# A hybrid decoder layer on one core: token sums in later heads, a fourth place for gate weight sums, closing steps beside the next head, scores two steps behind

## The chip, the core and the metric

The kernel runs on one core of a Trainium2 chip. A core has five engines that run beside each other, each with its own instruction order: TensorE (PE, matrix products into PSUM), VectorE (DVE), ScalarE (ACT), GpSimd (POOL) and SyncE (SP), whose queue issues nearly all DMA transfers here. An engine that waits for one instruction holds all that stand behind it. The metric is the device time of one execution in microseconds (us).

## What is computed

One layer of a decoder on 1024 tokens of width 1024, with 16 learned tokens put in front. Everything is float32. Two attention branches of four heads each read the same normalised rows; their outputs are gated, merged and projected, and a gated feed-forward part with a causal convolution follows:

```
h = concat(meta, x)                                   # 1040 rows
p = rms_norm(h) @ w_in + b_in                         # split into 13 parts
log_a = log_sigmoid(g_lr @ gla_w_gate + gla_b_gate) / 16
o_gla = head_rms(gla_chunked(g_q, g_k, g_v, log_a)) * silu(g_r)          # 4 heads
o_ml  = head_rms(mlstm_chunked(silu(conv(m_q, m_k)), m_v, m_i, m_f)) * sigmoid(m_o)   # 4 heads
h = h + (sigmoid(gate_a) * (o_gla @ w_bg) + sigmoid(gate_b) * (o_ml @ w_bm)) @ w_out
h = h + (silu(gate) * up) @ w_down,   gate, up = split(conv(rms_norm(h) @ w_up))
return rms_norm(h)[16:]
```

## The kernel before

**Products.** To keep float32 precision each operand is split into a high and a low part (`wH`, `wL`; `xH`, `xL`), and a product is three matmuls: high by high, high by low, low by high. ACT makes the high part with a copy, DVE the low part with a subtraction. The functions are `prep` (L99) for weights and `proj_cm` (L150) and `proj_v` (L176) for the projections: `proj_cm` goes in three pieces of 24 matmuls of some 346 columns (tile `pj`), `proj_v` in one short and eight long pieces of 24 matmuls of 256 columns (tile `pv`).

**Order.** The kernel is written against a layer that assigns buffers, places waits, and orders the instructions of each engine by priority and its own estimate of time, so an engine's order isn't that of the source. `issue_after` sets a lower bound for the place of an instruction. Buffers are named by tag; a tag with `bufs=2` has two places, and a new tile waits until the tile that had its place has been read by all its readers, DMA stores among them.

**Head stage.** There are eight heads, 0 to 3 of the first kind (`gla`, L570), 4 to 7 of the second (`mlstm`, L774). `head_proj(s)` (L417) makes the keys, queries and values of head s on PE. The rest of a head is a generator that `yield`s between its steps. `main` (L901) runs the projections, and for each projection piece it takes `PACE` = 1.7 steps from the list `side` (L888), so that a head's steps run beside the next head's projections. The loop at the end of the head stage is

```
main(head_proj(0))
for s in range(8):
    side.append((gla if s < 4 else mlstm)(s))
    if s > 3: token_sums(s - 4)
    if s < 7: main(head_proj(s + 1))
```

In `gla`, seven levels (`level`, L637) prepare decayed keys and queries `pk` for block sizes b = 1 to 64. A level has subtractions on DVE (L660, L661), an exponential on ACT (L662), products with the keys on POOL (L664, two for b under 32) and one with the queries on DVE (L665). Four small matmuls then give the scores of that level (`sc`, L601), which DVE copies under a mask (L618). In the source the scores of one level come after the next level. A head ends with `post` (L540): DVE scales the output rows `or` by a reciprocal root that POOL computes (L545), PE transposes them (`ot`, L554), ACT copies them to `of` (L556), and SP stores them to `osc`.

`token_sums(k)` (L456) makes on POOL four sums and differences of the input blocks (two of 1026 columns at L461, four of 514 at L466) and stores them to `tsc` (L468), for the gate stage. Its tiles `xa`, `xb` have the tag `r` (two places), `tx` the tag `gst` (one place).

**Gate stage.** The remaining projections (26 gates of 128 columns) are made in 13 rounds of two, each as a two by two block product with seven instead of eight block products (`piece`, L936; PSUM tiles Vg, Xg, Yg, Zg). `gate_weights(q)` (L984) loads the two weight blocks (`gw`), and makes their sums `gsA`, `gsB` and the high and low parts (`gHA`, `gLA`, `gHSA`, `gLSA`, `gHSB`, `gLSB`, `gA`) in four steps, which the loop takes one at a time. The parts A1, SA and SB take turns in three places in `wp`. The results of a round stand in `gu` (two places for each of the two gates). `gate_finish(q)` (L1039), called in round q + 1, loads the head outputs for gates of the first eight rounds (`go`, from `osc`, tag `o`, one place), applies silu or sigmoid on ACT (L1047), multiplies on DVE (L1048) and stores (`otd`); for the other gates it only stores. After each of the rounds 0 to 10 the loop calls `half_sums` (L1051) twice: it loads a quarter of a block of the down projection's weights (tile `ts`, tag `ts`, one place, two transfers), makes four differences on DVE (L1057) and stores them with two transfers (`tdn`, L1059), for the end of the kernel.

After that come the merge, the output projection, the feed-forward part (`up`, L933 again) and the down projection, which the change doesn't touch.

Of the kernel before, what the change touches and what calls it, by code (L numbers as in the profile page):

```python
# [9 lines left out]
F32 = mybir.dt.float32  # L10
# [7 lines left out]
P = 128  # L18
# [27 lines left out]
def hybrid_kernel(ctx, tc, x, meta, norm_mix, w_in, b_in, gla_w_gate, gla_b_gate, gla_norm,  # L46
# [370 lines left out]
    def head_proj(s):  # L417
        h = s % 4
        hh = heads.setdefault(s, {})
        bB = hd.tile([P, DV], F32, name=f"bB{s}", tag="bB", bufs=2)  # L420
        nc.sync.dma_start(bB, rowb(b_in, (O_GV if s < 4 else O_MV) + DV * h, DV))
        if s < 4:
            pk = key_proj(s) if s != 1 else iter(())
            qT = hh["q"] = hd.tile([P, T + 3], F32, name=f"qT{s}", tag="q", bufs=2)
            pq = proj_cm(uq[s], TH_POST if s else SEG_POST, T0, lambda p, t0, n: nc.scalar.activation(
                qT[:, t0:t0 + n], p, AF.Identity, bias=cc(C_GQ + h), scale=QS))
            if s == 0:
                yield from together(pk, pq, key_proj(1))
                yield from proj_cm(uk["lr"], TH_ALL, 0, lambda p, t0, n: nc.scalar.activation(
                    raw_s[0:96, t0:t0 + n], p[0:96, :], AF.Identity, bias=bsm[0:96]))  # L430
            else:
                yield from pk
                yield from pq
        else:
            kT = hd.tile([P, T + 3], F32, name=f"kT{s}", tag="k", bufs=2)
            qT = hd.tile([P, T + 3], F32, name=f"qT{s}", tag="q", bufs=2)
            hh["k"], hh["q"] = kT, qT
            for z, u, c in ((kT, uk[s], C_MK), (qT, uq[s], C_MQ)):
                nc.gpsimd.memset(z[:, 0:3], 0.0)
                yield from proj_cm(u, TH_ALL, 0, lambda p, t0, n, z=z, c=c: nc.scalar.activation(  # L440
                    z[:, 3 + t0:3 + t0 + n], p, AF.Identity, bias=cc(c + h)))
        vt = hd.tile([P, NC + 1, DV + 1], F32, name=f"v{s}", tag="v", bufs=2)
        if s >= 4:
            nc.gpsimd.memset(vt[:, :, DV:DV + 1], 1.0)
        hh["v"] = vt
        yield from proj_v(uv[s], bB, vt)
# [93 lines left out]
    def post(s, o, om, sc, ncols):  # L540
# [7 lines left out]
        yield  # L548
        for j in range(2):
            of = hd.tile([P, T], F32, name=f"of{s}_{j}", tag="of", bufs=2)  # L550
# [19 lines left out]
    def gla(s):  # L570
# [66 lines left out]
        def level(b):  # L637
# [18 lines left out]
            else:  # L656
# [6 lines left out]
                for e, k, _ in early:  # L663
                    nc.gpsimd.tensor_tensor(e, e, k, OP.mult)  # L664
# [3 lines left out]
        pk = level(1)  # L668
        yield
        yield  # L670
        for b in (2, 4, 8, 16, 32, 64):
            nk = level(b)
            if b == 64:
                yield
                turn()
                yield
                scores_diagonal()
                scores_large(pk, 32)
            else:
                scores_small(pk, b // 2)  # L680
            pk = nk
            yield
# [88 lines left out]
        yield from post(s, o, om[:, :DV], sc, [cc(C_GN + j) for j in range(2)])  # L771


    def mlstm(s):  # L774
# [110 lines left out]
        yield from post(s, o, om[:, :DV], sc, [cc(C_MN + 2 * h + j) for j in range(2)])  # L885


    side = []  # L888

    def advance():  # L890
        while side:
            try:
                next(side[0])
                return
            except StopIteration:
                side.pop(0)

    PACE = 1.7
# [13 lines left out]
    main(head_proj(0))  # L912
    for s in range(8):
        side.append((gla if s < 4 else mlstm)(s))
        if s == 3:
            side.append(small_rows())
        if s > 3:
            token_sums(s - 4)
        if s < 7:
            main(head_proj(s + 1))  # L920
    for j in TAIL:
        main(merge_gate_b(j))
    while side:
        advance()
# [59 lines left out]
    def gate_weights(q):  # L984
# [4 lines left out]
        sa, sb = (gs.tile([P, NK, P], F32, name=f"gs{x}{q}", tag=f"S{x}") for x in "AB")  # L989

# [4 lines left out]
        def two(src, name):  # L995
            h, l = (wp.tile([P, NK, P], F32R, name=f"g{p}{name}_{q}", tag="w" + p) for p in "HL")
            split(src, h, l)
            return [(h[:, 4 * i:4 * i + 4], l[:, 4 * i:4 * i + 4]) for i in range(2)]
        a = WP[q] = {}
        a["A11"], a["A12"] = two(rg, "A1")  # L1000
        yield
        nc.vector.tensor_tensor(sa[:, 0:4], ru[:, 0:4], ru[:, 4:8], OP.add)
        nc.vector.tensor_tensor(sa[:, 4:8], rg[:, 0:4], ru[:, 0:4], OP.subtract)
        a["S1"], a["S3"] = two(sa, "SA")
        yield
        nc.vector.tensor_tensor(sb[:, 0:4], sa[:, 0:4], rg[:, 0:4], OP.subtract)
        nc.vector.tensor_tensor(sb[:, 4:8], rg[:, 4:8], sb[:, 0:4], OP.subtract)
        a["S2"], a["S4"] = two(sb, "SB")
        yield
        t = gs.tile([P, NK, P], F32R, name=f"gA22_{q}", tag="A22")  # L1010
# [3 lines left out]

    wsteps = [gate_weights(q) for q in range(NG)]
# [35 lines left out]
    def half_sums(m, c):  # L1051
        t = gs.tile([P, 4, 256], F32, name=f"ts{m}{c}", tag="ts")
# [17 lines left out]
    weights_step(0)  # L1070
    u2 = wp.tile([P, T], F32, name="gu2", tag="gst", bufs=1)[:, :2 * W0].rearrange("p (a b) -> p a b", b=W0)
    behind_ = None
    for q in range(NG):
        gu[q] = [gs.tile([P, T], F32, name=f"gu{i}{q}", tag=f"u{i}", bufs=2) for i in range(2)]
        for p in range(2):
# [9 lines left out]
            if p == 0 and q:  # L1085
                weights_step(q)
                weights_step(q)
                gate_finish(q - 1)
# [660 lines left out]
```

## Time and profile before

| | us |
|---|---|
| three runs | 2021.89, 2028.81, 2032.42 (median 2028.81) |
| the profiled execution | 2011.35 |
| its span, first to last instruction | 2009.6 |
| mean granted TensorE clock | 0.976 of full speed |

In the rows of the profile "A <- B: t, n, longest" means that A sat idle t us in n places until B ended; a row of the timeline has start, duration, engine, line, operation, tiles, and in brackets the idle time before it and what ended it. SPq rows are the issues of transfers. A row of a stretch ("from:to length, ...") has the busy time and instructions of PE, weight loads, DVE, ACT and POOL, then the granted clock, the busy share of the DMA engines and GB/s.

### The profile page before, as it was taken

The page shows a single profiled execution, that of the slowest core. Times are in us where ns is not written, and L with a number is a line of the kernel's source. Part 1 is how long each engine was busy: PE and PEld are TensorE (multiplying, and loading weights), DVE is VectorE, ACT ScalarE, POOL GpSimd, SP SyncE. Part 2 cuts the span into 40 slices and gives each one's busy share as a digit, 9 for nine tenths or more (in the row PEclk, how much of TensorE's full clock was granted, in tenths as well). Part 3 has the DMA queues.
Part 4 walks back from the last instruction along what each step waited for, and adds up shares of the span by engine and source line. Part 5 has one row for each costly group of instructions (what it writes and reads, how often), then busy time and mean ns, then how long its engine had stood idle before and what let it go on. Part 6 is the DMA issues. An engine that isn't in the chain of part 4 may idle for free. (4 is left out here: it accounts for less than half of the span.)

```text
span 2009.6 us, 32599 instructions
## 1 busy us (share of the span) xinstructions
PE 1895.8 (94%) x13377; PEld 1807.0 (90%) x13377; DVE 1227.3 (61%) x1902; ACT 827.7 (41%) x1280; POOL 242.2 (12%) x213
## 2 busy tenths in 40 slices
PE   8699899889999998989999999999999999999998
PEld 8688888788999997988999999999999999987776
DVE  6163655756444266665543244778878887886767
ACT  5134444555433343332243133544444444455564
POOL 5610211200000000000000000002222322200000
PEclk8899999999999998999999999999999999999999
DMA  5311010212221277776584243333333333378794
GB/s 177 98 35 45 22 56 22 56 43 77 76 74 53 61 222 208 225 210 202 171 272 164 63 135 117 107 116 120 101 111 117 121 101 111 110 255 300 280 379 164
DMA packets 237376, 270.02 MB, mean 134 GB/s; under 512 B 13422, under 2 KB 195200, under 8 KB 237227
## 3 DMA queue, kind: packets, MB, share of 16 engines
q1 hardware_dynamic: 235387, 266.09, 41.2%
q8 instruction: 105, 1.72, 0.3%
q10 hardware_dynamic: 1840, 1.85, 0.3%
q14 instruction: 44, 0.36, 0.1%
HBM read 198.33 MB, written 69.57 MB: 133 GB/s over the span
## 5 line engine op out<-in xcount | busy, mean ns | idle before, releaser
L205 DVE TENSOR_TENSOR v<-pv,bB 128x256 f32<-128x256 f32 x64 | 27.0, 422 | 95.5 <-PE pv L201 95.4
L201 PE MATMUL pv<-wH_mv,xH 128*128 128x256 f32 x256 | 76.4, 298 | 0.0
L201 PE MATMUL pv<-wH_gv,xH 128*128 128x256 f32 x256 | 75.6, 295 | 0.0
L201 PE MATMUL pv<-wH_mv,xL 128*128 128x256 f32 x256 | 74.2, 290 | 0.0
L201 PE MATMUL pv<-wL_mv,xH 128*128 128x256 f32 x256 | 73.7, 288 | 0.0
L201 PE MATMUL pv<-wH_gv,xL 128*128 128x256 f32 x256 | 72.7, 284 | 0.0
L201 PE MATMUL pv<-wL_gv,xH 128*128 128x256 f32 x256 | 72.4, 283 | 0.0
L1396 PE MATMUL po<-wH_wo,yH 128*128 128x256 f32 x256 | 72.2, 282 | 0.1
L1396 PE MATMUL po<-wL_wo,yH 128*128 128x256 f32 x256 | 71.6, 280 | 0.3 <-DVE wL_wo L107 0.3
L1396 PE MATMUL po<-wH_wo,yL 128*128 128x256 f32 x256 | 71.8, 281 | 0.0
L664 POOL TENSOR_TENSOR pk<-pk,kT 128x256 f32<-128x256 f32 (+1 forms) x40 | 47.6, 1210 | 158.3 <-ACT pk L662 96.1
L1344 DVE SCALAR_TENSOR_TENSOR cv<-u,fc,cv 128x1024 f32<-128x1024 f32 x44 | 65.3, 1484 | 0.4
L1136 PE MATMUL bg<-ogH,wH_bg 128*128 128x342 f32 x192 | 61.5, 320 | 1.5 <-ACT gb L450 1.5
L1057 DVE TENSOR_TENSOR ts<-ts 128x256 f32<-128x256 f32 x88 | 37.1, 421 | 40.5 <-DMA ts<-in_ffn_w_down_dram 38.4
L1136 PE MATMUL bm<-omH,wH_bm 128*128 128x342 f32 x192 | 61.4, 320 | 0.0
L1136 PE MATMUL bg<-ogL,wH_bg 128*128 128x342 f32 x192 | 61.4, 320 | 0.0
L1136 PE MATMUL bm<-omH,wL_bm 128*128 128x342 f32 x192 | 61.3, 319 | 0.0
L1136 PE MATMUL bg<-ogH,wL_bg 128*128 128x342 f32 x192 | 61.3, 319 | 0.0
L1136 PE MATMUL bm<-omL,wH_bm 128*128 128x342 f32 x192 | 61.3, 319 | 0.0
L1309 POOL TENSOR_TENSOR SB<-SA,rg 128x512 f32<-128x512 f32 x20 | 32.1, 1607 | 235.9 <-issue 114.1
L933 PE MATMUL Xg<-TH,gLSB 128*128 128x258 f32 (+1 forms) x104 | 32.7, 315 | 25.6 <-DVE gLSB L993 25.4
L601 PE MATMUL sc<-pk 128*128 128x128 f32 x224 | 32.6, 291 | 24.2 <-POOL pk L664 12.3
(737 smaller groups left out, 7403.7 us busy)
## 6 DMA issues: line engine op xcount, KB each, us to landing
gw<-in_w_in_dram SPq DMA_DIRECT2D x26, 512.0 KB, 5.3
ts<-in_ffn_w_down_dram SPq DMA_DIRECT2D x44, 256.0 KB, 3.2
tdn<-ts SPq DMA_DIRECT2D x44, 256.0 KB, 4.3
rg<-in_ffn_w_up_dram SPq DMA_DIRECT2D x22, 512.0 KB, 3.7
ru<-in_ffn_w_up_dram SPq DMA_DIRECT2D x22, 512.0 KB, 3.6
adr<-s SPq DMA_DIRECT2D x40, 256.0 KB, 2.8
rd<-in_ffn_w_down_dram SPq DMA_DIRECT2D x20, 512.0 KB, 8.1
do<-tdn SPq DMA_DIRECT2D x18, 512.0 KB, 8.0
```

Of the source, the lines that this page charges most:

```text
L201: nc.tensor.matmul(pt[:, :DV], a[:, k, t0:t0 + P], b[:, k % 4, :], start=(i == 0), stop=(i == 3 * NK - 1))
L205: nc.vector.tensor_tensor(vt[:n, c, :DV], pt[:n, :DV], bB[:n, :], OP.add)
L601: nc.tensor.matmul(pt[:, i, :], pk[:, P * i:P * (i + 1)], pk[:, 512 + P * i:512 + P * (i + 1)], start=True, stop=True)
L664: nc.gpsimd.tensor_tensor(e, e, k, OP.mult)
L933: nc.tensor.matmul(out[:, :n], x[:, k, :], y[:, k, :], start=start and k == 0 and j == 0, stop=stop and k == 3 and j == 2, skip_group_chec ...
L1057: nc.vector.tensor_tensor(t[:, o], t[:, a], t[:, b], OP.subtract)
L1136: nc.tensor.matmul(pt[:, i, :n], a[:, k, :], b[k][:, t0:t0 + n], start=(k == 0 and j == 0), stop=(k == NK - 1 and j == 2))
L1309: late.tensor_tensor(sb[:, 0:4], sa[:, 0:4], rg[:, 0:4], OP.subtract)
L1344: nc.vector.scalar_tensor_tensor(y, u[:, j:SEQ + j], fc[:, j, jj:jj + 1], y, OP.mult, OP.add)
L1396: nc.tensor.matmul(pt[:, :DV], a, b[:, k % 4, :], start=(k == 0 and i == 0), stop=(k == NK - 1 and i == len(terms) - 1))
```

## The change

1. `head_proj` is cut in two. A head's own steps now begin after its keys and queries, beside its own values (`value_proj`) and the next head's keys and queries. `PACE` goes from 1.7 to 1.2.
2. `post` is no longer the end of a head's generator but goes to a second list, `closing`, from which each `advance` takes one step besides one of `side`. It has one empty step more, and `of` moves from tag `of` to tag `r`, where the token sums have their tiles.
3. `token_sums` is held back by `issue_after` behind the clearing of the query tile of heads 4 to 7.
4. In `gla` a level's scores come two levels later, and the second of the two early products goes to DVE.
5. In the gate stage every fourth of the parts A1, SA, SB gets a place of its own (`w4`), the sums are made in the loaded blocks instead of `gsA` and `gsB`, and the steps of a round's weights begin one half round earlier.
6. The tile of `half_sums` takes the tag `o` of `gate_finish`'s `go`.

```diff
--- before.py
+++ after.py
@@ -414,11 +414,9 @@
         return proj_cm(uk[s], TH_ALL if s > 1 else SEG_ALL, 0, lambda p, t0, n: nc.scalar.activation(
             kT[:, t0:t0 + n], p, AF.Identity, bias=cc(C_GK + s)))
 
-    def head_proj(s):
+    def key_query_proj(s):
         h = s % 4
         hh = heads.setdefault(s, {})
-        bB = hd.tile([P, DV], F32, name=f"bB{s}", tag="bB", bufs=2)
-        nc.sync.dma_start(bB, rowb(b_in, (O_GV if s < 4 else O_MV) + DV * h, DV))
         if s < 4:
             pk = key_proj(s) if s != 1 else iter(())
             qT = hh["q"] = hd.tile([P, T + 3], F32, name=f"qT{s}", tag="q", bufs=2)
@@ -436,13 +434,17 @@
             qT = hd.tile([P, T + 3], F32, name=f"qT{s}", tag="q", bufs=2)
             hh["k"], hh["q"] = kT, qT
             for z, u, c in ((kT, uk[s], C_MK), (qT, uq[s], C_MQ)):
-                nc.gpsimd.memset(z[:, 0:3], 0.0)
+                hh["mark"] = nc.gpsimd.memset(z[:, 0:3], 0.0)
                 yield from proj_cm(u, TH_ALL, 0, lambda p, t0, n, z=z, c=c: nc.scalar.activation(
                     z[:, 3 + t0:3 + t0 + n], p, AF.Identity, bias=cc(c + h)))
+
+    def value_proj(s):
+        bB = hd.tile([P, DV], F32, name=f"bB{s}", tag="bB", bufs=2)
+        nc.sync.dma_start(bB, rowb(b_in, (O_GV if s < 4 else O_MV) + DV * (s % 4), DV))
         vt = hd.tile([P, NC + 1, DV + 1], F32, name=f"v{s}", tag="v", bufs=2)
         if s >= 4:
             nc.gpsimd.memset(vt[:, :, DV:DV + 1], 1.0)
-        hh["v"] = vt
+        heads[s]["v"] = vt
         yield from proj_v(uv[s], bB, vt)
 
     def merge_gate_b(j, bank=None):
@@ -546,8 +548,9 @@
         nc.vector.tensor_scalar(om, om, sc[:2, 0:1], None, OP.mult)
         yield
         yield
+        yield
         for j in range(2):
-            of = hd.tile([P, T], F32, name=f"of{s}_{j}", tag="of", bufs=2)
+            of = hd.tile([P, T], F32, name=f"of{s}_{j}", tag="r", bufs=2)
             for gi in range(2):
                 tp = ps.tile([P, 4, P], F32, name=f"ot{s}_{j}_{gi}", tag="s", bufs=3)
                 for i in range(4):
@@ -660,26 +663,27 @@
                     nc.vector.tensor_tensor(e, t[..., b - 1:b].to_broadcast(t.shape), t, OP.subtract)
                 nc.vector.tensor_tensor(pl, b4[:, :, 1, :], ref, OP.subtract)
                 nc.scalar.activation(pk[:, :SEQ], pk[:, :SEQ], AF.Exp, scale=1.0 / 16)
-                for e, k, _ in early:
-                    nc.gpsimd.tensor_tensor(e, e, k, OP.mult)
+                for eng, (e, k, _) in zip((nc.gpsimd, nc.vector), early):
+                    eng.tensor_tensor(e, e, k, OP.mult)
             nc.vector.tensor_tensor(pl, pl, lv(qv, b)[:, :, 1, :], OP.mult)
             return pk
 
-        pk = level(1)
-        yield
-        yield
-        for b in (2, 4, 8, 16, 32, 64):
-            nk = level(b)
-            if b == 64:
-                yield
-                turn()
-                yield
-                scores_diagonal()
-                scores_large(pk, 32)
-            else:
-                scores_small(pk, b // 2)
-            pk = nk
+        made = []
+        for b in (1, 2, 4, 8, 16, 32, 64):
+            made.append((b, level(b)))
+            if len(made) > 2:
+                c, pk = made.pop(0)
+                scores_small(pk, c)
             yield
+        yield
+        c, pk = made.pop(0)
+        assert c == 32
+        turn()
+        yield
+        scores_diagonal()
+        scores_large(pk, 32)
+        (_, pk), = made
+        yield
 
 
         kh = wtile(f"kh{s}")
@@ -768,7 +772,7 @@
                 nc.scalar.activation(junk[:, :DV], o(c), AF.Square, accum_out=ss[:, c + 1:c + 2])
             yield
         sc = rstd_of(ss, DV, NC + 1, hd, f"rs{s}")
-        yield from post(s, o, om[:, :DV], sc, [cc(C_GN + j) for j in range(2)])
+        closing.append(post(s, o, om[:, :DV], sc, [cc(C_GN + j) for j in range(2)]))
 
 
     def mlstm(s):
@@ -882,20 +886,27 @@
         nc.vector.tensor_tensor(ss, ss, rc, OP.mult)
         sc = rstd_of(ss, DV, NC + 1, hd, f"rs{s}")
         nc.vector.tensor_tensor(sc, sc, rc, OP.mult)
-        yield from post(s, o, om[:, :DV], sc, [cc(C_MN + 2 * h + j) for j in range(2)])
-
-
-    side = []
+        closing.append(post(s, o, om[:, :DV], sc, [cc(C_MN + 2 * h + j) for j in range(2)]))
+
+
+    side, closing = [], []
+
+    def step(gens):
+        if gens:
+            try:
+                next(gens[0])
+            except StopIteration:
+                gens.pop(0)
+                return False
+        return True
 
     def advance():
-        while side:
-            try:
-                next(side[0])
-                return
-            except StopIteration:
-                side.pop(0)
-
-    PACE = 1.7
+        step(closing)
+        while side and not step(side):
+            pass
+
+
+    PACE = 1.2
     due = [0.0]
 
     def main(gen, pace=PACE):
@@ -909,18 +920,20 @@
     NP2 = NJ // 2
     tdn = [dram.tile([NP2, P, 2, 512], F32, name=f"tdn{i}") for i in range(2)]
 
-    main(head_proj(0))
+    main(key_query_proj(0))
     for s in range(8):
         side.append((gla if s < 4 else mlstm)(s))
         if s == 3:
             side.append(small_rows())
         if s > 3:
-            token_sums(s - 4)
+            with tc.issue_after(heads[s]["mark"].ins):
+                token_sums(s - 4)
+        main(value_proj(s))
         if s < 7:
-            main(head_proj(s + 1))
+            main(key_query_proj(s + 1))
     for j in TAIL:
         main(merge_gate_b(j))
-    while side:
+    while side or closing:
         advance()
     heads_ctx.close()
 
@@ -986,32 +999,43 @@
         rg, ru = (wp.tile([P, NK, P], F32, name=f"gw{i}{q}", tag="wr", bufs=2) for i in range(2))
         for r, g in ((rg, GATES[2 * q]), (ru, GATES[2 * q + 1])):
             nc.sync.dma_start(r, wsrc(w_in, 0, NK, g[0], P))
-        sa, sb = (gs.tile([P, NK, P], F32, name=f"gs{x}{q}", tag=f"S{x}") for x in "AB")
-
         def split(src, h, l):
             nc.scalar.activation(h, src, AF.Copy)
             nc.vector.tensor_tensor(l, src, h.bitcast(F32), OP.subtract)
 
-        def two(src, name):
-            h, l = (wp.tile([P, NK, P], F32R, name=f"g{p}{name}_{q}", tag="w" + p) for p in "HL")
-            split(src, h, l)
-            return [(h[:, 4 * i:4 * i + 4], l[:, 4 * i:4 * i + 4]) for i in range(2)]
+        def place(name):
+            nonlocal ngw
+            ngw += 1
+            if ngw % 4 == 0:
+                return [gs.tile([P, NK, P], F32R, name=f"g{p}{name}_{q}", tag="w4" + p) for p in "HL"]
+            return [wp.tile([P, NK, P], F32R, name=f"g{p}{name}_{q}", tag="w" + p) for p in "HL"]
+
+        def halves(t):
+            return [(t[0][:, 4 * i:4 * i + 4], t[1][:, 4 * i:4 * i + 4]) for i in range(2)]
         a = WP[q] = {}
-        a["A11"], a["A12"] = two(rg, "A1")
-        yield
-        nc.vector.tensor_tensor(sa[:, 0:4], ru[:, 0:4], ru[:, 4:8], OP.add)
-        nc.vector.tensor_tensor(sa[:, 4:8], rg[:, 0:4], ru[:, 0:4], OP.subtract)
-        a["S1"], a["S3"] = two(sa, "SA")
-        yield
-        nc.vector.tensor_tensor(sb[:, 0:4], sa[:, 0:4], rg[:, 0:4], OP.subtract)
-        nc.vector.tensor_tensor(sb[:, 4:8], rg[:, 4:8], sb[:, 0:4], OP.subtract)
-        a["S2"], a["S4"] = two(sb, "SB")
-        yield
-        t = gs.tile([P, NK, P], F32R, name=f"gA22_{q}", tag="A22")
+        t = place("A1")
+        split(rg, *t)
+        a["A11"], a["A12"] = halves(t)
+        yield
+        s3 = gs.tile([P, 4, P], F32, name=f"gS3{q}", tag="S3")
+        nc.vector.tensor_tensor(s3, rg[:, 0:4], ru[:, 0:4], OP.subtract)
+        nc.vector.tensor_tensor(ru[:, 0:4], ru[:, 0:4], ru[:, 4:8], OP.add)
+        a["S1"], a["S3"] = halves(place("SA"))
+        split(ru[:, 0:4], *a["S1"])
+        split(s3, *a["S3"])
+        yield
+        nc.vector.tensor_tensor(rg[:, 0:4], ru[:, 0:4], rg[:, 0:4], OP.subtract)
+        nc.vector.tensor_tensor(rg[:, 4:8], rg[:, 4:8], rg[:, 0:4], OP.subtract)
+        t = place("SB")
+        split(rg, *t)
+        a["S2"], a["S4"] = halves(t)
+        yield
+        t = gs.tile([P, NK, P], F32R, name=f"gA22{q}", tag="A22")
         a["A22"] = t[:, 0:4], t[:, 4:8]
         split(ru[:, 4:8], *a["A22"])
         yield
 
+    ngw = 0
     wsteps = [gate_weights(q) for q in range(NG)]
 
     def weights_step(q):
@@ -1049,7 +1073,7 @@
             nc.sync.dma_start(otd[g][j], u[:, :NP])
 
     def half_sums(m, c):
-        t = gs.tile([P, 4, 256], F32, name=f"ts{m}{c}", tag="ts")
+        t = gs.tile([P, 4, 256], F32, name=f"ts{m}{c}", tag="o")
         for k in range(2):
             nc.sync.dma_start(t[:, 2 * k:2 * k + 2], w_dn[P * (2 * m + k):P * (2 * m + k + 1), :].rearrange(
                 "p (i n) -> p i n", i=2)[:, :, 256 * c:256 * c + 256])
@@ -1067,7 +1091,6 @@
             weights_step(0)
     for j in COVER:
         main(merge_gate_b(j, gate_bank(f"pc{j}")))
-    weights_step(0)
     u2 = wp.tile([P, T], F32, name="gu2", tag="gst", bufs=1)[:, :2 * W0].rearrange("p (a b) -> p a b", b=W0)
     behind_ = None
     for q in range(NG):
@@ -1082,10 +1105,11 @@
                 weights_step(q + 1)
             if behind_:
                 next(behind_)
-            if p == 0 and q:
+            if p == 0:
                 weights_step(q)
-                weights_step(q)
-                gate_finish(q - 1)
+                if q:
+                    gate_finish(q - 1)
+                weights_step(q + 1)
             next(g)
             behind_ = g
         if q < NP2:
```

## The prediction

> **What bounds the kernel now.** I read the page first, then PE's own waits, then the two places that these name.
>
> ```profile
> span 2009.6 us, 32599 instructions
> PE 1895.8 (94%) x13377; PEld 1807.0 (90%) x13377; DVE 1227.3 (61%) x1902; ACT 827.7 (41%) x1280; POOL 242.2 (12%) x213
> ...
> PE Xg L933 <- DVE gLSB L993: 25.4, 8, 6.9
> PE pj L158 <- ACT kT L414: 16.4, 1, 16.4
> PE ot L554 <- DVE or L545: 12.6, 5, 6.0
> PE sc L601 <- POOL pk L664: 12.3, 8, 3.1
> PE sc L601 <- DVE pk L665: 9.3, 8, 2.1
> ...
> PE sc L601 <- DVE A L588: 2.0, 2, 1.8
> ...
> PE Yg L933 <- DVE TL L1028: 1.9, 1, 1.9
> ...
> PE Yg L933 <- ACT TH L1027: 1.8, 1, 1.8
> ```
>
> PE sets the pace: 94% busy, 113.8 us idle. The waits are a list of what can be had: 16.4 us once in the head stage, 36.2 us spread over it (12.6 + 12.3 + 9.3 + 2.0), 25.4 us in the gate stage, 3.7 us at its start. The work of PE is the same before and after, so the change can win little more than these 82 us and the slow clock behind them. The first place is the single wait:
>
> ```profile
> 75.24 0.32 SPq L468 DMA_DIRECT2D tsc<-xb  x1
> 75.66 0.39 SPq L102 DMA_DIRECT2D wr_gq<-in_w_in_dram  x1
> ...
> 80.96 1.06 ACT L106 ACTIVATE wH_gq<-wr_gq 128x1024 fp32r<-128x1024 f32 x1 [24.05 <-DMA wr_gq<-in_w_in_dram]
> ...
> 82.43 0.66 PE L158 MATMUL pj<-xH,w_lr 128*128 128x346 f32 x1 [16.37 <-ACT kT L414]
> ```
>
> Although the program asks for token sums at heads 4 to 7, they run at 40 to 91 us. SP's queue is in order: the load of head 1's query weights stands behind stores that wait for POOL, ACT stands at the split of these weights, and behind that split stands the eviction that PE needs.
>
> The second place is the gate stage. These are SP's issues in one round (a pair of gates), DVE's longest wait, and mean rounds:
>
> ```profile
> 801.10 1.26 SPq L1054 DMA_DIRECT2D ts<-in_ffn_w_down_dram  x2
> ...
> 806.87 1.49 SPq L1059 DMA_DIRECT2D tdn<-ts  x2
> 808.41 0.60 SPq L1046 DMA_DIRECT2D go<-oscg  x1
> 811.17 1.25 SPq L1054 DMA_DIRECT2D ts<-in_ffn_w_down_dram  x2
> ...
> 819.68 0.57 SPq L1059 DMA_DIRECT2D tdn<-ts  x1
> 820.30 0.72 SPq L1046 DMA_DIRECT2D go<-oscg  x1
> 825.34 1.73 SPq L1054 DMA_DIRECT2D ts<-in_ffn_w_down_dram  x2
> ...
> 789.99 0.43 DVE L1057 TENSOR_TENSOR ts<-ts 128x256 f32<-128x256 f32 x1 [7.25 <-DMA ts<-in_ffn_w_down_dram]
> ...
> 732.95:903.27 170.32, 149.96 (x1178) 148.16 (x1177) 108.32 (x197) 54.11 (x73) 0.00 (x0) 0.93 0.72 212
> 903.27:974.03 70.76, 63.91 (x506) 63.32 (x505) 42.62 (x83) 18.17 (x27) 0.00 (x0) 0.95 0.68 202
> ...
> 854.28:874.70 20.42, 20.36 (x170) 20.16 (x169) 15.24 (x27) 7.46 (x11) 0.00 (x0) 1.00 0.70 204
> ```
>
> The first window is seven rounds, so 24.3 us each; the last is one round in which PE hardly waited, 20.4 us, what a round costs when PE alone sets it. One tile `ts` (one buffer) carries load, four subtractions, two stores; the next load waits for the stores to land. Two uses make 801.10 to 825.34, 24.2 us: the round is that chain. PE's wait for gLSB is its shadow: DVE runs in order and stands at a `ts` subtraction (7.25 us) with gLSB behind it.
>
> **The change part by part.**
>
> *Token sums.* In the order of the changed program the query weights' load of head 1 comes right after head 0's value weights, and POOL's first token sum stands among head 3's last levels. That removes the 16.4 us. Behind such a gap PE runs at half clock for a while:
>
> ```profile
> 791.60 0.58 PE L933 MATMUL Xg<-TH,gLSB 128*128 128x258 f32 x1 [6.94 <-DVE gLSB L993]
> ...
> 795.00:797.00 2.00, 2.00 (x11) 2.00 (x11) 0.73 (x3) 0.39 (x1) 0.00 (x0) 0.50 1.03 298
> 797.00:800.00 3.00, 3.00 (x26) 3.00 (x26) 1.63 (x3) 1.06 (x1) 0.00 (x0) 0.95 1.13 246
> ...
> 65.42 2.35 POOL L461 TENSOR_TENSOR xa<-xH,xL 128x1026 f32<-128x1026 f32 x1 [1.66 <-DMA tsc<-xa]
> ...
> 70.03 1.27 POOL L466 TENSOR_TENSOR tx<-xa 128x514 f32<-128x514 f32 x1
> ```
>
> From 791.6 to 797 at half clock loses 2.7 us of work; I take 2.4 here, so **-18.8** in all. The moved sums cost 2 x 2.35 + 4 x 1.27 = 9.8 us of POOL each, four times, in heads where POOL is near idle; their 16 stores now stand on SP ahead of later heads' weights, at places where those weights are needed more than 20 us later. Counted 0; without that cover one head's 9.8 us shows. The `r` buffers that the sums now share with `of` can hold ACT at an `of` copy for some 8 us in head 5 (an estimate from the sums' durations and the landing of a store); PE then runs value projections, which DVE evicts. Also 0.
>
> *Heads: closing steps beside the next levels, scores two steps back, half of the early products on DVE.*
>
> ```profile
> L664 POOL TENSOR_TENSOR pk<-pk,kT 128x256 f32<-128x256 f32 (+1 forms) x40 | 47.6, 1210 | 158.3 <-ACT pk L662 96.1 <-issue 62.1
> ...
> L665 DVE TENSOR_TENSOR pk<-pk,qT 128x512 f32<-128x512 f32 x28 | 26.2, 939 | 0.1
> ...
> L660 DVE TENSOR_TENSOR pk<-bc 128x256 f32<-128x256 f32 (+1 forms) x40 | 23.0, 601 | 0.0
> L618 DVE COPY_PREDICATED A<-mu,sc 128x512 f32<-128x512 uint8 x20 | 19.2, 958 | 1.3 <-PE sc L601 1.2
> L661 DVE TENSOR_TENSOR pk<-bc 128x512 f32<-128x512 f32 x24 | 18.2, 758 | 0.0
> ```
>
> A small level costs DVE 2 x 0.60 + 0.76 + 0.94 + 0.96 = 3.9 us, and 0.6 more for the product taken from POOL, where two took 2 x 1.2. Between two score products the changed order has about 24 projection matmuls and eight small ones, an estimated 3.5 us, so DVE is slightly behind for five levels; two steps of lag give 7 us to absorb it. At best all 36.2 us go, at worst DVE's backlog gives half back and the transposes still wait: -36 to -10. I take three quarters, **-28** with the clock.
>
> *The gate stage: a fourth place, no S tiles, `ts` put into the buffer `o`.* The fourth place and steps made a round earlier take gLSB off PE's path. But half_sums now uses the one buffer that gate_finish uses for `go`. In the changed order of SP's queue a round reads: `ts` load, two `tdn` stores, `ts` load, two `tdn` stores, `go`, `otd`, `go`, `otd`; each load waits for what the use before it leaves. Before, the two `go` loads ran beside the `ts` chain (808.41 and 820.30 lie inside it). Now they stand in it. Their price:
>
> ```profile
> L1048 DVE TENSOR_TENSOR gu<-gu,go x16: 1218/1222/1228, 743.6 to 925.2; 128x1026 f32<-128x1026 f32 x16
> ...
> DMA to landing us min/median/max: 5.8/6.7/7.6
> ...
> DMA to landing us min/median/max: 4.5/5.3/6.2
> ...
> 933.42 1.39 SPq L1054 DMA_DIRECT2D ts<-in_ffn_w_down_dram  x2
> ...
> 976.66 1.25 SPq L1054 DMA_DIRECT2D ts<-in_ffn_w_down_dram  x2
> ```
>
> A `go` lands after 5.8 to 7.6 us in today's traffic; the second landing row is that of the equally large `gw`, 4.5 at least. With 1.2 for the product and 0.5 for the hand-over, one `go` costs 6.2 to 9.3; with fewer transfers at once I take 6.6. A `ts` use without `go` beside it takes (976.66 - 933.42) / 4 = 10.8. A round is 2 x 10.8 + 2 x 6.6 = 34.8 us. Bounds: 29.6 (two `ts` at 10.1, the quicker of the two shown, 801.10 to 811.17; two `go` at 4.7, little more than the shortest landing) and 42.8 (two `ts` at 12.1, half of today's 24.2; two `go` at 9.3). I take the value near the lower end, because a chain in series meets fewer transfers. gate_finish for gates with a silu or sigmoid is in rounds 1 to 8, so 8 x (34.8 - 24.3) = **+84** (42 to 148). PE cannot run ahead of it: the evictions of round q stand in DVE's order between the `ts` subtractions and the `go` products, and `gu` has two buffers. In the rounds after that the pair of `ts` takes 21.6 against 23.6 today, and the last have none: **-4**. The gate stage starts better, since head 7 closes three thirds of a projection earlier and frees the places of the token blocks: **-4** (3.7 us waited, and a little clock).
>
> Sum: -18.8 - 28 + 84 - 4 - 4 = +29 us, so 2011.35 becomes 2040 in a profiled execution of that kind (span 2009.6, 1.75 us around it). The three runs shown have a median of 2028.81; the same ratio, 1.0144, gives **2058**.
>
> A rule against the change stands in the Trainium skill, "TensorE: Matmul & The Clock Gate", section "Part 1: The HAM clock gate": an idle window of about 3.4 us halves PE's clock, and it takes as long of sustained work to get it back. The trace agrees: half clock behind the 6.94 us gap, for 5.4 us. By the rule a round with three such gaps loses about 5 us of PE time; at 20.4 us of work in 34.8 that fits in, and the sum stays.
>
> **Rivals.**
>
> *The buffer does not pace.* If a `go` can be loaded before the last `tdn` has landed, or DVE's order lets evictions pass, a round stays at 24.3 or nears 20.4. It decides as soon as a `go` load is issued within 4 us of a `ts` load. Then the heads' gain stands alone: -18.8 - 28 - 4 = -51, 1978 on the median's scale, faster. For it: today's rounds hide `go`. Against: one buffer, four uses, and the order of the queue.
>
> *Short transfers.* The same chain at its low bound, if serial transfers land as fast as the fastest of today: rounds of 29.6, +42 in place of +84, with the rest -13, 2016; up to 2028 with rounds of 31.
>
> *PE cold and heads that keep their waits.* Gaps of 5 to 9 us in every round hold PE at half clock; a whole cold round is up to 2 x 20.4 = 40.8, and rounds of 38 add 8 x 3.2 = 26; half of the heads' 28 lost adds 14: 2098. That the scores do not lag as stated is ruled out by PE's order, where two levels lie between.
>
> **How the numbers follow.** The forecast has 0.60 (2035 to 2085), no pacing 0.13, short transfers 0.14, cold 0.13. The range 2005 to 2105 leaves out the first rival and the ends of the others, about 0.2. Half a per cent, 10 us, is what a measurement of this kernel tells from no change. Faster: 0.13 and half of the short transfers, 0.20. Same: the rest of them and the forecast's lower edge, 0.15. Slower: 0.65.
>
> **What would show it.** Right: PE's wait on kT at 66 to 82 us gone; rounds of 33 to 37 us in the gate stage with `go` issued only after `tdn` landed, DVE's longest waits there on `go` and `ts`, a granted clock there well under 0.93; waits of `sc` and `ot` under 10 us together. Wrong: rounds near 24 us or less, or PE waits in the heads as large as now.

## The result, and the profile after

| | us |
|---|---|
| before, median of 20 runs (lowest, highest) | 2029.51 (2021.89, 2035.9) |
| after, median of 20 runs (lowest, highest) | 2035.01 (2026.21, 2040.9) |
| after to before | 1.0033, 95% interval 1.002 to 1.0045 |
| the profiled execution after, its span, its clock | 2030.93, 2028.9, 0.971 |

The change costs a third of a per cent, some 6 us. The prediction had 2058 and slower by more than half a per cent as the likeliest. The profiled execution of before (2011.35) lies under all 20 of its timed runs, so the spans of the two profiles differ by 19 us where the kernels differ by 6. Below, times of parts come from the profiles, and what an edit is worth comes from ratios of timed runs; one per cent is 20.3 us, a ratio's interval is about 0.0025 to either side, 5 us, and that of a difference of two ratios 5 to 7 us.

The page's first lines and PE's waits after, in the form in which the prediction shows those of before:

```profile
span 2028.9 us, 32590 instructions
PE 1895.7 (93%) x13377; PEld 1809.9 (89%) x13377; DVE 1246.3 (61%) x1931; ACT 823.0 (41%) x1291; POOL 238.7 (12%) x197
...
PE Vg L946 <- ACT gu L965: 55.6, 5, 13.3
PE sc L604 <- DVE pk L668: 12.9, 9, 3.4
...
PE k0t L813 <- ACT of L559: 5.4, 1, 5.4
PE Yg L946 <- ACT gHSA L1003: 5.3, 2, 5.0
PE sc L604 <- DVE A L621: 4.5, 4, 1.8
```

PE does the same work (1895.7 us against 1895.8). The waits on `kT` (16.4 us), `or` (12.6) and `gLSB` (25.4) are gone. A new one is twice as large as any of them: 55.6 us on the eviction of a gate's first product, in five places. There is also a wait of 5.4 us of a head's transposed key on the copy to `of`, of which more below.

The gate stage from its first eviction of `Vg` to that of the thirteenth round, in the row of a stretch, first before, then after:

```profile
714.37:995.02 280.65, 251.59 (x1981) 249.01 (x1982) 179.17 (x319) 86.75 (x116) 0.41 (x1) 0.94 0.71 206
```

```profile
688.12:724.61 36.49, 34.77 (x278) 34.77 (x279) 23.60 (x44) 10.11 (x19) 0.00 (x0) 0.95 0.59 168
724.61:929.39 204.78, 145.38 (x1116) 143.95 (x1114) 104.60 (x189) 53.19 (x75) 0.00 (x0) 0.85 0.56 156
929.39:1010.45 81.06, 73.26 (x577) 71.93 (x577) 41.29 (x84) 15.95 (x31) 0.00 (x0) 0.94 0.68 182
688.12:1010.45 322.33, 253.41 (x1969) 250.65 (x1969) 169.49 (x315) 79.25 (x124) 0.00 (x0) 0.88 0.59 164
```

The stage begins 26.3 us earlier and lasts 41.7 us longer. Counted by these evictions, its three parts after are two rounds of 18.2 us, six of 34.1, four of 20.3. ACT's evictions of the first half of a round (258 columns; x2 is two evictions in one row) say where the parts part; the bracket is what each waited for:

```profile
688.12 0.38 ACT L965 ACTIVATE gu<-Vg 128x258 f32<-128x258 f32 x1
704.53 0.39 ACT L965 ACTIVATE gu<-Vg 128x258 f32<-128x258 f32 x1 [1.06 <-PE Vg L946]
724.61 0.39 ACT L965 ACTIVATE gu<-Vg 128x258 f32<-128x258 f32 x1 [0.92 <-PE Vg L946]
755.09 0.39 ACT L965 ACTIVATE gu<-Vg 128x258 f32<-128x258 f32 x1 [8.97 <-DMA otdg<-gu]
...
893.66 0.66 ACT L965 ACTIVATE gu<-Vg 128x258 f32<-128x258 f32 x2 [5.31 <-DMA otdm<-gu]
929.39 0.66 ACT L965 ACTIVATE gu<-Vg 128x258 f32<-128x258 f32 x2 [6.34 <-DMA otdm<-gu]
951.22 0.66 ACT L965 ACTIVATE gu<-Vg 128x258 f32<-128x258 f32 x2 [3.51 <-DMA gsca<-gu]
965.57 0.39 ACT L965 ACTIVATE gu<-Vg 128x258 f32<-128x258 f32 x1 [1.29 <-DMA otdm<-gu]
```

The first three evictions wait for nothing or for PE. From 755 on they wait for a store out of `gu`: both places of `gu` are taken, and a place comes free when the gate of an earlier round has got its `go` and is stored. PE itself is ahead of these evictions. Its first matmuls of the first and of the fourth round are

```profile
681.28 0.28 PE L946 MATMUL Vg<-xH,gHA 128*128 128x258 f32 x1
...
743.04 0.28 PE L946 MATMUL Vg<-xH,gHA 128*128 128x258 f32 x1
...
858.70 0.58 PE L946 MATMUL Vg<-xH,gHA 128*128 128x258 f32 x1 [12.11 <-ACT gu L965]
```

so its first three rounds took 20.6 us each, its own pace; the 18.2 is short only because the very first eviction (688.12) came late. The last row is how PE is held later: `Vg` of a round waits until that of the round before has been evicted from its one place in PSUM. One round of SP's queue, without the `gw` loads:

```profile
825.92 1.32 SPq L1078 DMA_DIRECT2D ts<-in_ffn_w_down_dram  x2
832.48 1.97 SPq L1083 DMA_DIRECT2D tdn<-ts  x2
836.40 1.25 SPq L1078 DMA_DIRECT2D ts<-in_ffn_w_down_dram  x2
...
843.62 0.57 SPq L1083 DMA_DIRECT2D tdn<-ts  x1
848.30 0.33 SPq L1070 DMA_DIRECT2D go<-oscm  x1
...
853.42 0.42 SPq L1070 DMA_DIRECT2D go<-oscm  x1
860.60 0.32 SPq L1073 DMA_DIRECT2D otdm<-gu  x1
860.96 1.32 SPq L1078 DMA_DIRECT2D ts<-in_ffn_w_down_dram  x2
```

The four uses of the one place follow each other: 10.5 and 11.9 us for the two `ts`, 5.1 and 7.5 for the two `go`, 35.0 in all. `go` is issued 4.7 us after the last `tdn`, when that has landed, and PE sits still for 12 us at the end of this round (the row at 858.70).

### The profile page after: what moved, and what is told of

Same layout as the page of the kernel before. It is cut to its first block, busy times and chain, and to the rows that moved or that the text cites. A ratio compares the mean times of both kernels' runs of the same rounds, so it can differ in the third digit from the quotient of the medians.

```text
span 2028.9 us, 32590 instructions
## 1 busy us (share of the span) xinstructions
PE 1895.7 (93%) x13377; PEld 1809.9 (89%) x13377; DVE 1246.3 (61%) x1931; ACT 823.0 (41%) x1291; POOL 238.7 (12%) x197
## 5 line engine op out<-in xcount | busy, mean ns | idle before, releaser
L946 PE MATMUL Vg<-xH,gHA 128*128 128x258 f32 (+1 forms) x104 | 31.8, 306 | 55.6 <-ACT gu L965 55.6
L946 PEld LDWEIGHTS Vg<-xH,gHA 128*128 128x128 f32 x104 | 21.3, 205 | 56.6 <-ACT gu L965 56.6
L1315 POOL TENSOR_TENSOR A<-u2raw,A 128x512 fp32r<-128x512 f32 x20 | 43.8, 2191 | 91.5 <-ACT A L1314 89.4
```

Of the source, the lines that this page charges most:

```text
L946: nc.tensor.matmul(out[:, :n], x[:, k, :], y[:, k, :], start=start and k == 0 and j == 0, stop=stop and k == 3 and j == 2, skip_group_chec ...
L1315: eng.tensor_tensor(l, src, h.bitcast(F32), OP.subtract)
```

## The experiments

**First the two halves of the diff and the disputed place.** Four kernels: one tag changed, the head stage alone, the gate stage alone, the hold alone.

*e1: the changed kernel, with a place of its own for `ts`.*

```diff
-        t = gs.tile([P, 4, 256], F32, name=f"ts{m}{c}", tag="o")
+        t = gs.tile([P, 4, 256], F32, name=f"ts{m}{c}", tag="ts")
```

> The changed kernel with one word put back: the tile of half_sums has its own tag ts again, so that go and ts no longer share a place. Theory (one place paces): rounds fall from 34.9 us to the pair of ts uses, 21 to 22 us, or to PE's own 20.4; twelve rounds take 250 to 265 us instead of 322, PE's wait of 55.6 us for gu goes to under 5, and the time is 55 to 65 us below the changed kernel's: ratio to before 0.970 to 0.977. Rival (the order of SP's queue or DVE's order paces, not the place): rounds stay over 28 us and the ratio over 0.99.

Measured 0.9824 (0.9798 to 0.985), 1993.86 us. The place alone is worth 1.0033 - 0.9824, 42 us, and PE's wait of 55.6 us on the eviction of `Vg` is gone. The ratio lies between my two expectations, since the rounds are not at PE's pace. The row of the gate stage, and PE's longest wait:

```profile
689.11:975.42 286.31, 255.18 (x1990) 249.92 (x1991) 176.03 (x330) 77.39 (x124) 0.40 (x1) 0.94 0.70 192
```

```profile
PE Yg L946 <- ACT gHSA L1003: 23.1, 7, 5.7
```

12 rounds in 286.3 us are 23.9 each, about those of before (280.65 / 12 = 23.4). The wait that the weights' sums caused has only another name: 23.1 us for `gHSA` where it was 25.4 for `gLSB`.

*e2: the head stage of the changed kernel with the gate stage of before (items 1 to 4 of the change).* *e3: the reverse (items 5 and 6).* The cut is at the line that sets the gate blocks' widths, `W0, W1 = 258, 256`. In short, e2 against the changed kernel, then e3 against it:

```diff
-        t = gs.tile([P, 4, 256], F32, name=f"ts{m}{c}", tag="o")
+        t = gs.tile([P, 4, 256], F32, name=f"ts{m}{c}", tag="ts")
...
-            if ngw % 4 == 0:
-                return [gs.tile([P, NK, P], F32R, name=f"g{p}{name}_{q}", tag="w4" + p) for p in "HL"]
...
```

```diff
-    PACE = 1.2
+    PACE = 1.7
...
-            with tc.issue_after(heads[s]["mark"].ins):
-                token_sums(s - 4)
+            token_sums(s - 4)
...
```

> The head stage as changed, the gate stage as before. Theory: the 27 us by which the gate stage began earlier in the changed kernel's profile (681 instead of 708 us) go through to the end: ratio 0.985 to 0.989. Rival: the profiled execution of before (2011 us, its timed runs 2022 to 2036) was a lucky one and the timed runs lose elsewhere what this shows, or the gate stage gives part back: ratio 0.990 to 0.996.

> The gate stage as changed, the head stage as before. Theory: full rounds of 34 to 36 us, twelve rounds 320 us instead of 281, so 35 to 42 us longer: ratio 1.017 to 1.021. Rival (the chain was late in the changed kernel only because the token sums were stored late): rounds under 30 us, ratio under 1.01.

Measured 0.981 (0.9786 to 0.9834) for the heads alone and 1.0296 (1.0272 to 1.032) for the gate stage alone: -39 and +60 us, each beyond what I had expected. e1 and e2 differ by 3 us, in favour of the old gate stage and within the interval: no gain from the fourth place, the missing S tiles and the earlier steps is seen there. The halves add up to +22 where both together give +7, so 15 us are a matter of how they meet.

*e4: the kernel before with the token sums held back, and nothing else.*

```diff
-                nc.gpsimd.memset(z[:, 0:3], 0.0)
+                hh["mark"] = nc.gpsimd.memset(z[:, 0:3], 0.0)
...
-        token_sums(s - 4)
+        with tc.issue_after(heads[s]["mark"].ins):
+            token_sums(s - 4)
```

> The kernel before with one part of the change: the token sums held back to heads 4 to 7. Theory: PE's wait of 16.4 us for kT and the slow clock after it go, 18 to 19 us, and nothing comes back: ratio 0.990 to 0.992. Rival: the sums cost as much on POOL, SP and the shared places in the later heads as they cost early: ratio 0.996 to 1.002.

Measured 0.9913 (0.989 to 0.9936), -18 us. PE's wait on `kT` is gone, and the others of the head stage stand about as they were (`or` 15.3 us, `pk` 12.0 and 10.8; before 12.6, 12.3 and 9.3). That leaves 0.9913 - 0.981, 21 us, for the rest of the head stage's change.

**Then the chain in the place, and the wait on `of`.**

*e5: the changed kernel with two places of the tag `o`.* *e6: the same two places in the gate stage of before, behind the changed heads.* *e7: the kernel before with `ts` put in the place of `go`, nothing else.* *e8: e5, and `of` back under its own tag.*

```diff
 e5, e6 (in e6 the tag of ts was "ts")
-            o = gs.tile([P, T], F32, name=f"go{q}_{i}", tag="o")
+            o = gs.tile([P, T], F32, name=f"go{q}_{i}", tag="o", bufs=2)
-        t = gs.tile([P, 4, 256], F32, name=f"ts{m}{c}", tag="o")
+        t = gs.tile([P, 4, 256], F32, name=f"ts{m}{c}", tag="o", bufs=2)
 e7
-        t = gs.tile([P, 4, 256], F32, name=f"ts{m}{c}", tag="ts")
+        t = gs.tile([P, 4, 256], F32, name=f"ts{m}{c}", tag="o")
 e8, besides
-            of = hd.tile([P, T], F32, name=f"of{s}_{j}", tag="r", bufs=2)
+            of = hd.tile([P, T], F32, name=f"of{s}_{j}", tag="of", bufs=2)
```

> The changed kernel with two places of tag `o` in place of one, shared by `go` and `ts` as before. Theory (the chain of loads, products and stores in the one place paces the gate stage, also with `ts` alone in its own place): two places halve the chain, 34.8 / 2 = 17.4 us, under the 20.4 us that PE needs, so rounds of 21 to 22 us in place of the 24 to 26 of e1, 10 rounds times 3 = 30 us less: ratio to the kernel before 0.965 to 0.970, and PE's wait for gHSA (23.1 us in e1) under 8. Rival (with the place taken out, the weights' sums on DVE and ACT set the round): rounds stay at 24 or more, 0.979 to 0.984.

> Head stage of the changed kernel, gate stage of the kernel before (three places for the weights' sums, the S tiles, the later steps), but `go` and `ts` share two places. Theory (the fourth place and the earlier steps are worth something only when the chain of the `ts` tile no longer paces): 10 to 20 us slower than e5, with PE waiting 15 us or more for gLSB or gLSA. Rival (they are worth nothing): within 5 us of e5. If the chain was not what paced e2, the time stays at that of e2, 0.981.

> The kernel before with one edit: the tile of the differences takes the tag `o`, in one place, together with `go`. Theory (the shared place alone makes the loss of the gate stage): as e3, ratio 1.025 to 1.035, full rounds of 33 to 38 us. Rival (the new steps of the weights cost part of e3's loss, since DVE and ACT now do them earlier in the round): 1.010 to 1.020.

> e5, and `of` goes back to the tag `of`, away from the token sums. Theory (the wait of PE's keys on the copy to `of`, 5.4 us in the changed kernel, is the hold by the token sums in the shared places): that wait goes, 4 to 8 us less than e5. Rival (the tag `of` is also the place of the tile KT of the next head, and the closing steps that now run beside that head hold it): a wait of the same or larger size at the next head's first steps, no gain or up to 15 us slower than e5.

| | ratio to before | 95% interval | gate stage, 12 rounds, us |
|---|---|---|---|
| e5 two places | 0.9776 | 0.9753 to 0.9799 | 273.95 |
| e6 two places, old weight steps | 0.9752 | 0.9739 to 0.9765 | 270.08 |
| e7 sharing alone | 1.0233 | 1.0212 to 1.0254 | 339.36 |
| e8 two places, `of` apart | 0.9687 | 0.9669 to 0.9706 | 277.97 |

e5 takes 10 us off e1, not the 30 that I expected. The difference, with its interval, is 3 to 17 us. The wait for `gHSA` is down from 23.1 to 0.7 us, so the chain of the `ts` tile was what stood behind it, but rounds come to 22.8 us, and PE now waits in small pieces for DVE's evictions (PE's waits in e5):

```profile
...
PE Yg L946 <- DVE gu L974: 6.9, 4, 3.4
PE Yg L946 <- DVE gu L980: 6.2, 5, 2.4
PE k0t L813 <- ACT of L559: 5.6, 1, 5.6
...
PE Zg L946 <- DVE gu L975: 4.0, 3, 2.0
PE Zg L946 <- DVE gu L981: 3.9, 3, 1.8
```

e6 answers whether the fourth place was only covered by the chain: no. With the chain loosened, three places and the old steps are not slower than four and the new ones, and PE waits 6.0 us for `gLSA`, and for `gLSB` 2.4 where e2 has 17.9, not 15 or more. e7 fell between what I wrote for the theory and for the rival: +47 us of e3's +60 come from the one tag; about 13 (intervals of 5 on each) are left for the new weight steps in the same stage. With the new heads the same steps cost nothing that shows (e1 against e2), and no run says why they do with the old.

In e7 the paced stage is 58.7 us longer than before, and in the changed kernel 41.7. The issue of the first `ts` load and the first eviction show a difference, e7 first:

```profile
721.62 0.38 ACT L952 ACTIVATE gu<-Vg 128x258 f32<-128x258 f32 x1
...
724.46 6.54 SPq L1054 DMA_DIRECT2D ts<-in_ffn_w_down_dram  x2
```

```profile
676.98 2.77 SPq L1078 DMA_DIRECT2D ts<-in_ffn_w_down_dram  x2
```

With the old heads the chain begins 2.8 us behind the first eviction (in e3 too: 721.87 against 719.09), with the new ones 11.1 us ahead of it (688.12). A chain that paces the stage and starts 14 us earlier would end that much earlier. This fits the 15 us between the sum of the halves and the whole, but it is an argument from the traces: no run varied the start alone, and in the profiles e3's gate stage is 24.5 us longer than that of the changed kernel, whose code there is the same.

e8 is 18 us faster than e5, where I had expected 4 to 8. The rows of the changed kernel in which the wait arises, by engine:

```profile
521.71 2.81 POOL L463 TENSOR_TENSOR xb<-xH,xL 128x1026 f32<-128x1026 f32 x1 [17.51 <-DVE v L205]
...
528.02 0.32 SPq L470 DMA_DIRECT2D tsc<-xa  x1
...
531.51 1.27 ACT L559 ACTIVATE of<-ot,col 128x512 f32<-128x512 f32 x2 [8.17 <-DMA tsc<-xa]
...
525.52 0.41 DVE L205 TENSOR_TENSOR v<-pv,bB 128x256 f32<-128x256 f32 x1
531.53 0.22 DVE L564 TENSOR_SCALAR of<-otm,col 128x2 f32<-128x2 f32 x1 [5.60 <-DMA tsc<-xa]
531.66 0.41 DVE L205 TENSOR_TENSOR v<-pv,bB 128x256 f32<-128x256 f32 x1
...
532.25 0.38 PE L813 MATMUL k0t<-ident,kc 128*16 128x128 f32 x1 [5.44 <-ACT of L559]
```

`of` takes the place of the token sum `xa`, which is stored only at 528.0, behind POOL's late sums. ACT stands 8.2 us at the copy. DVE stands beside it, 5.6 us at its own small write into the same tile, with an eviction of the value projection (`v`, 531.66) behind it. So PE has nothing to fall back on: by their tags, the transposes (`s`, three places) need a place in PSUM that waits for these copies, and the values (`pj`, three places) one that waits for DVE. Behind the gap the clock is at half:

```profile
526.00:532.00 6.00, 0.81 (x7) 0.60 (x6) 0.47 (x2) 0.49 (x1) 3.26 (x3) 0.78 0.34 132
532.00:536.00 4.00, 3.75 (x19) 3.51 (x20) 2.05 (x6) 0.78 (x2) 0.00 (x0) 0.50 0.71 158
536.00:540.00 4.00, 4.00 (x34) 3.86 (x34) 1.38 (x2) 0.00 (x0) 0.00 (x0) 0.98 0.68 104
```

5.4 us of gap and about 2 of half clock explain some 7 of the 18. In e5 PE is idle for 40.1 of the first 700 us and in e8 for 30.6 (700 less the busy time of fourteen stretches of 50 us), with the waits of `sc` on `pk` smaller too (10.0 against 13.6).

**Last, the best combination, the one tag, and the two parts of the levels.**

*e9: e6 with `of` apart.* *e10: the changed kernel with `of` apart, everything else as changed.* Both have the last edit of e8.

> The kernel of e6 (head stage of the changed kernel, gate stage of before, two places shared by `go` and `ts`) with `of` back under its own tag. Theory (the effects are separate: two places take the chain off the path, `of` in the place of the token sums costs 12 to 18 us, the fourth place and the earlier steps bring nothing): e6 less 12 to 18 us, ratio 0.966 to 0.970, at or under e8's 0.9687. Rival (the fourth place is needed as soon as the gate stage begins earlier): above e8 by 5 us or more, with PE waiting over 12 us for gLSA, gLSB or gHSA.

> The changed kernel with `of` back under the tag `of`, `ts` still in the one place of `go`. Theory (the head stage is 12 to 18 us longer for the shared `of`, whatever the gate stage does): ratio 0.994 to 0.998 where the changed kernel has 1.0033, the wait of the keys on the copy to `of` gone, rounds as in the changed kernel. Rival (the chain in the one place starts when it did, so an earlier gate stage only waits longer for it): 1.001 to 1.004 and rounds 10 us or more longer in sum.

e9: 0.9664 (0.9642 to 0.9687), 1961.23 us, the fastest kernel of the study, 68 us under before and 74 under after. e10: 0.9966 (0.9951 to 0.9981). Both came out as the theory had it: `of` in the token sums' place costs 0.0067 to 0.0089, 14 to 18 us, in all three pairs (e10, e8, e9). In e10 the gate stage keeps its length and only begins earlier (at 674.21):

```profile
674.21:997.04 322.83, 253.69 (x1969) 250.79 (x1969) 169.57 (x315) 79.29 (x123) 0.00 (x0) 0.89 0.60 163
```

Against the changed kernel, e10's first eviction of the keys is 4.4 us earlier in heads 4 and 5, 1.5 in head 6, 8.8 in head 7 (558.47 against 567.29), and the gate stage begins 13.9 us earlier. The hold shown above lies between the keys of heads 6 and 7 and has its 7.3 us there; 4.4 come ahead of head 4, where the longest wait of `sc` on `pk` falls from 3.4 to 2.1 us, and the cause of the rest stays open.

*e11: e9 with the scores one level behind.* *e12: e9 with both early products on POOL.*

```diff
 e11
-            if len(made) > 2:
+            if len(made) > 1 and b != 64:
 e12
-                for eng, (e, k, _) in zip((nc.gpsimd, nc.vector), early):
-                    eng.tensor_tensor(e, e, k, OP.mult)
+                for e, k, _ in early:
+                    nc.gpsimd.tensor_tensor(e, e, k, OP.mult)
```

> The kernel of e9 with the scores one level behind, as before. Theory (the second step of lag hides DVE's products): PE's waits of `sc` return to about the 21.6 us that the kernel before has (12.6 in e8), 8 to 14 us slower than e9. Rival (DVE falls behind over a whole head, so that one step or two make no difference): within 4 us of e9.

> The kernel of e9 with both early products of a level on POOL, as before. Theory (with two steps of lag the 1.2 us more on POOL are hidden, and DVE has 0.6 us less per level): within 4 us of e9, or up to 6 us faster. Rival (POOL's second product is what ends the scores' wait, as 12.3 us in the kernel before): waits of `sc` on POOL of 8 to 12 us, 8 to 14 us slower.

e11: 0.9662 (0.9635 to 0.9689). e12: 0.9661 (0.9637 to 0.9685). e9 has 0.9664, so neither edit alone makes a difference that shows. The waits of `sc`, of e9, e11 and e12 in this order:

```profile
PE sc L604 <- DVE pk L668: 10.3, 7, 2.1
...
PE sc L604 <- DVE A L621: 1.6, 3, 0.5
```

```profile
PE sc L604 <- DVE pk L668: 12.9, 11, 2.1
```

```profile
PE sc L604 <- DVE pk L668: 8.2, 4, 2.1
...
PE sc L604 <- DVE A L621: 5.7, 3, 3.0
```

12 to 14 us of waits remain in all three, and with the early product on either engine it is DVE that ends them. What is left of the heads' gain then belongs to the other parts, the closing steps beside the next levels and the earlier start of a head's steps. That is by elimination and not shown: neither part was put back alone, and with both edits at once, which was not run either, the two steps of lag and the product on DVE could still stand in for each other.

## Why the prediction was wrong

The terms, with what the runs measured for each (ratios times 2029.5 us):

| term | predicted, us | measured, us | from |
|---|---|---|---|
| token sums held back | -18.8 | -18 | e4 |
| heads, the rest, and the better start of the gate stage | -28 - 4 | -21 | e2 less e4 |
| of which: `of` in place `r` | 0 | +14 to +18 | e10, e8, e9 |
| of which: without it | -32 | -35 to -39 | the row above taken off |
| `ts` in the place of `go`, and the rounds after | +84 - 4 | +42 | after less e1 |
| fourth place, earlier steps | no term | +3 | e1 less e2 |
| sum | +29 | +6 | after: +7 |

- **The step that failed** is "8 x (34.8 - 24.3) = +84". The mechanism was right and so was the length of a round: 34.1 us in the mean of the paced rounds against 34.8, in the order and with the waits that the prediction had named. Wrong was the count, and with it "PE cannot run ahead of it". e1 differs from the changed kernel in the place alone; its rows for the same two, six and four rounds are

```profile
689.11:726.89 37.78, 36.06 (x289) 36.04 (x290) 25.43 (x49) 10.00 (x18) 0.00 (x0) 0.95 0.69 196
726.89:877.13 150.24, 129.95 (x1009) 126.77 (x1008) 91.77 (x168) 44.27 (x69) 0.00 (x0) 0.94 0.74 198
877.13:975.42 98.29, 89.18 (x694) 87.11 (x695) 58.83 (x116) 23.12 (x40) 0.40 (x1) 0.94 0.64 180
```

The place thus costs -1.3, +54.5 and -17.2, together 36 us of these profiles, where the timed runs have 42. Only six rounds were paced. Ahead of them PE made three rounds at its own pace before the places of `gu` and PSUM were full. In the six it did 1116 matmuls, 107 more than in e1, and in the last four 117 fewer (by the record, in which some can be missing): a round has 168, so it was ahead of the evictions by some two thirds of a round. The eviction at 951.22 waited for a store that needs no `go` (`gsca`), the held one after it followed in 14.4 us, and the rounds came at 20.3 where e1 has 24.6. Against before, whose first two rounds took 41.6 us, the middle six 147.3 and the last four 91.7 (from 714.37 by its evictions), the parts are -5, +57.5 and -10.6; of the -5 there, 3.8 are in e1 too and are the better start, for which the prediction had its own -4.
- **Token sums:** confirmed on its own, to a microsecond, with an interval of 5.
- **`of` and the token sums in one tag:** the hold was foreseen in size and place ("some 8 us in head 5"; it is 8.17), and priced at 0, because "PE then runs value projections, which DVE evicts". DVE was held by the same tile. A cover was named without asking whether it stood behind the same wait. The miss is 14 to 18 us, of which this hold makes some 7; a smaller part shows ahead of head 4, and the rest was not found.
- **The heads' -28:** that the sum, -21, came near is luck: two errors nearly cancel, the one just named and a gain about as large as all the waits of 36.2 us, of which three quarters were counted. The reason given for it does not stand as far as it was tried: in e9 one step of lag does as well as two (e11), and both products on POOL do as well as one (e12). The prediction asked for `sc` and `ot` waits under 10 us together; `ot` went to none, `sc` stayed at 17.4 after and at 12 in e9.
- **Fourth place and earlier steps:** thought to take `gLSB` off PE's path. (The steps come half a round earlier, not a round, as it says there.) They bring no gain that shows (e1 against e2, e5 against e6), and the chain of the `ts` tile, not the number of places, stood behind that wait: two places for that tile take it from 17.9 (e2) to 2.4 us (e6). The prediction had read just that from DVE's 7.25 us at a `ts` subtraction, and then did not use it.
- **The rivals:** "the buffer does not pace" is out, by e1 and by the paced rounds. "Short transfers" gave 2016 to 2028 by rounds of 29.6 to 31, which are not what happened: the time lands near theirs by fewer paced rounds, not by shorter ones. "PE cold" is out: the rounds are 34.1 us and not 38, and the granted clock in the six paced rounds is 0.85; behind the gap of 12.78 us that ends at 894.10 it is 0.50 up to 897 and 0.88 in the next 4 us. Its other half did come in part, since `sc` kept its waits.

The Trainium skill's rule of the clock, "TensorE: Matmul & The Clock Gate", section "Part 1: The HAM clock gate", by which an idle window of about 3.4 us halves the clock, agrees with the trace here too: 0.50 in the 4 us behind a gap of 5.44 us. The return to full clock took longer than the equal time of work that the prediction drew from the same rule: 5.4 us behind the gap of 6.94 us in the profile before.

## What to carry to other kernels

A stage that one buffer paces does not cost rounds times the excess: PE runs free until the buffers behind it are full, and catches up when the pacing ends, so count the rounds between these two points (here six of the eight) and take off what PE has done ahead. Before a stall is called covered, look whether the engine that covers it touches the same tile; here one late store held ACT and DVE at once, and PE with them. And two uses that each seem small enough for one place make a chain in series: two places shared by the same four uses were better than one place for each kind by 10 us (e5 against e1, interval 3 to 17).

## What the runs showed of the hardware

Executions of one kernel differ by more than a step of such a change: 20 runs of before lie between 2021.89 and 2035.9 us, and the profiled one took 2011.35. A sum made against a single execution has to be carried over to the timed runs, as the prediction did with a ratio. Where the 18 us of that execution come from stays open.
